# The gated group formed second in two mixer passes, and smaller portions of beside-work

## The chip, the cores and the metric

One core of a Trainium2 chip runs the whole program in one launch. The metric is the device time in microseconds (us) of that core; lower is better. A core has five engines with queues of their own: TensorE (PE in the profile, with its weight loads as PEld), VectorE (DVE), ScalarE (ACT), GpSimd (POOL) and SyncE (SP), which here only issues DMAs. Each engine takes its instructions strictly in the order of its queue.

## The reference

One layer of a hybrid encoder over 2048 prompt tokens and 32 tokens of a running stream. Cut to what matters here:

```python
h = rms_norm(x, g_mix); p = h @ w_in            # 1024 -> 2048 columns, eight groups of 256
ya = pool_mixer(seg[0], ...)                    # trailing windows 2/4/8/16, mean - self
z  = seg[1] * sigmoid(seg[2])                   # the gated group ("glu")
c  = causal_depthwise(z, w_dw, 31 taps) + b_dw
yb = silu(layer_norm(c))
yc = seg[4] * causal_depthwise(seg[5] * seg[3], w_sconv, 3 taps)
yd = seg[6] * chunk_mlp(seg[7])                 # v: mixed over positions in chunks of 128
x  = x + concat(ya, yb, yc, yd) @ w_out
x  = x + (silu(f @ w_gate) * (f @ w_up)) @ w_down     # f = rms_norm(x, g_ffn)
y  = rms_norm(x, g_final)
```

All numbers are fp32. A product of two fp32 numbers is formed from a high and a low part of each, with three matmuls.

## The kernel before, in words

**Tiles.** The 2080 tokens are five chunks (`c` = 0 to 4) of `C` = 416. The mixers run in three passes over them, `PASSES = ((0,), (1, 2), (3, 4))`; p is the pass. Then comes the feed-forward part, which the change does not touch. A *product* is one output tile of 128 columns by 416 tokens: 8 slices of the 1024 inputs, three matmuls each (L230 hi·whi, L231 hi·wlo, L232 lo·whi). The mixers have 120 products: 80 of the input projection, and 40 of `w_out`. I number them P0 to P119 in the order in which TensorE does them; pass 1 starts with P16, its products go chunk by chunk. A group of columns is two products per chunk (four in passes 1 and 2; `in_short`, `in_glu` have two pairs, so eight). Each weight of 128 columns is loaded by SP (L136), cut into `whi` by ACT (L137) and `wlo` by POOL (L138); three such pairs fit.

**Groups.** In passes 1 and 2 each group is a function: `in_v` (the last group, and the start of the generator `spatial`: transposes `tp` L620, ACT copies `vt` L624, matmuls `mx` L631, DVE sums L645), `in_short`, `in_pool` (starts `pooling`), `in_glu` (the gated group: sigmoid `g` L571 on ACT, product `z` L574 on DVE; then the generator `taps`), and `in_gates` (which takes up the results of the others). Before, pass 1 has the order v, short, pool, glu, gates, that is P16–19, P20–27, P28–31, P32–39, P40–47; then `w_out` of pass 0 is P48–55. Pass 2 has v P56–59, pool P60–63, glu P64–71, short P72–79, gates P80–87; then come `w_out` of pass 1 (P88–103) and of pass 2 (P104–119).

**Beside-work.** Generators hold the work that is not a matmul of a product: `taps(p, z)` (60 instructions of DVE at L726, 30 taps for each of two tiles, 128x416 in pass 0, 128x832 in pass 1 and 128x862 in pass 2), `normed_silu` (per chunk, after the taps: sum `sm` L738 on DVE, `total` L742 on PE, L746 on DVE, squares on ACT L755, `tok` L147 on PE, `ms` on DVE, a power `rt` L163 on POOL, then, in passes 0 and 1, a round trip through DRAM, `line` L185 and `rs` L187 on SP's queue, then L773 on DVE and the silu L776 on ACT), `pooling`, `short_conv`, `stats(c)` (loads of `xt`, L791, and their squares on ACT, L794: what the norm of chunk c needs), `normed(c)` (forms the chunk's `hi` and `lo`, loading `xk`, L436; DVE's are L211 and L207, ACT's L214), and for `w_out` `mixed_parts`. After every product `fill(budget)` runs steps of the first three started generators, and after them of `spare`, where the taps are; each step has a cost, and `fill` stops when the budget is spent. `need(...)` runs a generator to its end on the spot.

**Order.** DVE and PE do their instructions in the order in which the program writes them (`MANUAL`); those of ACT, POOL and SP are put in an order by the scheduler when the kernel is built. So `fill` and `need` set how much of the taps stands between which products in DVE's queue, and where PE's `total`, `tok` and `mx` stand between products.

**What ties glu to the taps.** The gated `z` has one buffer, so `in_glu(p)` begins with `need(("taps", p - 1))`: what is left of the taps of the pass before goes into DVE's queue in one piece. `w_out_pass` adds each product to `x2` on DVE (L376); `ps` has five buffers, so PE can be four products ahead of DVE. `ps_ax`, for the small matmuls, has three.

Of the kernel before, what the change touches and what calls it, by code (L numbers as in the profile page):

```python
# [79 lines left out]
def width(p, h):  # L80
    n0, n1 = tail(p)
    return h + n0 + (h + n1 if n1 else 0)
# [3 lines left out]
def trunk_kernel(ctx: ExitStack, tc: tile.TileContext, a):  # L86
# [40 lines left out]
    def weight(pool, src, lo_eng, cuts=1, between=None, raw=None):  # L127
        hi = pool.tile([P, KT, P], F32R, tag="whi", name="whi")
        lo = pool.tile([P, KT, P], F32R, tag="wlo", name="wlo")
        hf, lf = (t.rearrange("p k m -> p (k m)") for t in (hi, lo))  # L130
        if raw is None:
            raw = wts.tile([P, D], F32, tag="raw", name="raw", bufs=2)
        n = D // cuts
        for q in range(cuts):
            o = slice(q * n, (q + 1) * n)
            nc.sync.dma_start(out=raw[:, o], in_=src[:, o])  # L136
            nc.scalar.copy(out=hf[:, o], in_=raw[:, o])  # L137
            lo_eng.tensor_sub(out=lf[:, o], in0=raw[:, o], in1=hf[:, o].bitcast(F32))  # L138
            if between:
                between(q)  # L140
        return hi, lo
# [96 lines left out]
    def ktiles(pair):  # L238
        hi, lo = pair
        return [(hi[:, k], lo[:, k]) for k in range(KT)]  # L240
# [18 lines left out]
    def fill(budget):  # L259
        budget -= debt[0]  # L260
        late = []
        i = 0
        while budget > 0 and i < min(active[0], len(ahead)):
            step = next(ahead[i], DONE)
            if step is DONE:
                ahead.pop(i)
            elif step is WAIT or step is LATE:
                if step is LATE:
                    late.append(ahead[i])
                i += 1  # L270
            else:
                budget -= step
        while budget > 0 and spare:
            step = next(spare[0], DONE)
            if step is DONE:
                spare.pop(0)
            elif step is WAIT:
                break
            else:
                budget -= step  # L280
        for g in late:
            while (step := next(g, DONE)) is not WAIT:
                if step is DONE:
                    ahead.remove(g)
                    break
                budget -= step
        debt[0] = max(-budget, 0.0)
# [3 lines left out]
    def need(*names):  # L291

        for name in names:
            for _ in made[name]:
                pass

    def start(name, gen, spot=None):
        made[name] = gen
        ahead.insert(len(ahead) if spot is None else spot, gen)
# [63 lines left out]
    def w_out_pass(p, then=()):  # L363
        chunks = PASSES[p]
        order = (4, 5, 6, 7, 0, 1, 2, 3)
        for m0 in range(0, KT, 2):
            w = {m: ktiles(weight(wts, a["w_out"][m], nc.gpsimd)) for m in (m0, m0 + 1)}
            for c in chunks:
                need(("mixed", c))
                for m in w:  # L370
                    ps = ps_mm.tile([P, 512], F32, tag="mm", name="ps")
                    product(ps[:, :C], [w[m][k] for k in order], [mh[c][k] for k in order])
                    if (c, m) in then:
                        then[c, m]()
                    fill(3.7)
                    nc.vector.tensor_add(out=x2[c][:, m], in0=ps[:, :C], in1=x2[c][:, m])  # L376
            yield

    with ExitStack() as st:
# [99 lines left out]
        def project(p, h, *ms, w=None, pre=(), then=()):  # L479

            w = dict(w or {})
            for m in ms:
                if m not in w:
                    w[m] = ktiles(weight(wts, a["w_in"][m], nc.gpsimd))
            for c in PASSES[p]:
                if c:
                    need(("h", c))
                for m in ms:
                    if (c, m) in pre:
                        ps = pre[c, m]  # L490
                    else:
                        ps = ps_mm.tile([P, 512], F32, tag="mm", name="ps")
                        product(ps[:, :C], w[m], h[c])
                        if (c, m) in then:
                            then[c, m]()
                        fill(2.8 if p == 0 else 3.7)
                    yield c, m, ps[:, :C]

        def in_v(p, products):
            chunks = PASSES[p]  # L500
            n0, n1 = tail(p)
            v = segp.tile([P, 2, HV + width(p, 0)], F32, tag="seg", name="v", bufs=2)
            if chunks[0] * C % P:
                halo(v, "v", HV, p)
            for c, m, ps in products:
                o = HV + (c - chunks[0]) * C
                plain(v[:, m - 14, o : o + C], ps, c)
            keep(v, "v", HV, p)
            if n1:
                nc.scalar.dma_start(out=a["o_v"], in_=v[:, :, HV + n0 :])  # L510
            for c in chunks:
                mix[c] = bigp.tile([P, KT, C], F32, tag="big", name="mix")
            start(("spatial", p), spatial(p, v))
# [41 lines left out]
        def in_glu(p, h, **pre):  # L555
            if p > 1:
                need(*(("normed", c) for c in PASSES[p - 2]))
            if p:
                need(("taps", p - 1))
            z = segp.tile([P, 2, width(p, 30)], F32, tag="z", name="z")  # L560
            halo(z, "conv", 30, p)
            for t in range(2):
                for c, m, ps in project(p, h, 4 + t, 2 + t, **pre):
                    if m >= 4:
                        g = row("g")
                        if c == 0:
                            times_r(g, ps, c)
                            nc.scalar.activation(out=g, in_=g, func=AF.Sigmoid)
                            times_r(g, g, c)
                        else:  # L570
                            nc.scalar.activation(out=g, in_=ps, func=AF.Sigmoid)  # L571
                        continue
                    for s, d, n in conv_pieces(p, 30, c):
                        nc.vector.tensor_mul(  # L574
                            out=z[:, t, s : s + n], in0=ps[:, d : d + n], in1=g[:, d : d + n]
                        )
            states(z, "conv", 30, p)
            made["taps", p] = taps(p, z)
            spare.append(made["taps", p])

        def in_pool(p, h):
            need(("pooling", 1) if p == 2 else ("spatial", p))
            pz = segp.tile([P, 2, width(p, 15)], F32, tag="seg", name="pz", bufs=2)
            halo(pz, "pool", 15, p)
            for c, t, ps in project(p, h, 0, 1):
                for s, d, n in conv_pieces(p, 15, c):
                    if c == 0:
                        nc.vector.tensor_mul(
                            out=pz[:, t, s : s + n], in0=ps[:, d : d + n], in1=rfirst[:, d : d + n]
                        )  # L590
                    else:
                        nc.scalar.copy(out=pz[:, t, s : s + n], in_=ps[:, d : d + n])
            states(pz, "pool", 15, p)
            start(("pooling", p), pooling(p, pz))
# [187 lines left out]
        h = {}  # L782
        rt = {}

        def stats(c):

            rt[c] = rowp.tile([P, NTB], F32, tag="rt", name="rt", bufs=6)
            for js in ((0, 1, 2), (3,)):
                xt = bigp.tile([P, KT * C], F32, tag="big", name="xt")
                for i, j in enumerate(js):  # L790
                    nc.sync.dma_start(out=xt[:TB, i * D : (i + 1) * D], in_=a["xt"][c, j])  # L791
                for i, j in enumerate(js):
                    xj = xt[:TB, i * D : (i + 1) * D]
                    nc.scalar.activation(out=xj, in_=xj, func=AF.Square, accum_out=rt[c][:TB, j : j + 1])  # L794
                    yield WAIT
            rsqrt_of([rt[c][:TB]], 1.0 / D, rt=rt[c])
            yield WAIT
# [40 lines left out]


        in_v(1, project(1, h, 14, 15))  # L840
        start(("stats", 3), stats(3))
        in_short(1, h)
        start(("stats", 4), stats(4))
        in_pool(1, h)
        in_glu(1, h)
        need(("pooling", 0), ("normed", 0), ("stats", 3), ("stats", 4))
        in_gates(1, h, {
            (1, 13): lambda: (start(("mixed", 0), mixed_parts(0), 0), start(("h", 3), normed(3), 0)),
# [3 lines left out]


        in_v(2, project(2, h, 14, 15))
        in_pool(2, h)
        in_glu(2, h)
        in_short(2, h)
        whole.add(0)
        start(("fstats", 0), ffn_stats(0))
# [795 lines left out]
```

## Time and profile before

| | |
|---|---|
| time, median of 3 runs | 2127.08 us (2125.25 to 2128.69) |
| profiled execution | 2125.5 us; its span in the trace 2123.8 us |
| busy share of the span | PE 95%, PEld 93%, DVE 68%, POOL 54%, ACT 36% |
| mean granted TensorE clock | 0.982 |
| mixers, 0 to about 658 us | of 117 to 658 us PE is busy 519 us |
| feed-forward, 658 to 2124 us | PE busy 1415.5 of 1466 us |

The profile shows one execution. Its times count from the start of the span. The views used below are: the timeline (start, length, engine, line, operation, tiles, number of instructions; in square brackets how long the engine had been idle and what ended it), the list of waits, groups of instructions (busy time, mean of one, idle time before), the chain of work that ended last, and the table of stretches (for each: busy us of PE, PEld, DVE, ACT and POOL with the number of instructions, then the granted clock, the DMA share, GB/s).

### The profile page before, as it was taken

What the parts mean: (1) busy time and instruction counts of PE and PEld (TensorE: products, weight loads), DVE (VectorE), ACT (ScalarE), POOL (GpSimd) and SP (SyncE); (2) the same over time, 40 slices, a digit from 0 to 9 for tenths busy, and PEclk for the clock granted to TensorE, in tenths of its full rate; (3) what the DMA queues carried; (4) which work ended last, traced back from release to release, by engine and by line L of the source; (5) the groups of instructions that cost most, each with busy time, mean ns of one, the idle gap of its engine ahead of it and who ended that gap; (6) DMA issues with size and microseconds to landing.
All of it is one profiled execution on the core that took longest, in us unless ns stands there. A gap on an engine that the chain in (4) does not pass through costs nothing.

```text
span 2123.8 us, 31916 instructions
## 1 busy us (share of the span) xinstructions
PE 2027.5 (95%) x11902; PEld 1980.8 (93%) x11902; DVE 1444.6 (68%) x2207; ACT 767.5 (36%) x1472; POOL 1138.5 (54%) x891
## 2 busy tenths in 40 slices
PE   8699998999997999999999999999999999999997
PEld 7689997899897999999998999999998999999997
DVE  3896599499576677556557676787557577656555
ACT  5423232332334333333334343333334333333332
POOL 2523352243335655656668565666667556655664
PEclk9899998999998999999999999999999999999998
DMA  7634233113367445222224534543224534422221
GB/s 214 177 94 112 71 116 112 41 61 124 108 168 206 137 136 153 85 71 78 78 99 146 188 97 128 159 151 124 75 86 148 195 103 136 133 70 75 75 80 59
DMA packets 152011, 247.88 MB, mean 117 GB/s; under 512 B 23440, under 2 KB 101008, under 8 KB 151216
## 3 DMA queue, kind: packets, MB, share of 16 engines
q1 hardware_dynamic: 149136, 245.67, 37.4%
q8 instruction: 94, 1.54, 0.3%
q14 instruction: 61, 0.50, 0.1%
q10 hardware_dynamic: 2720, 0.18, 0.1%
HBM read 209.42 MB, written 36.36 MB: 116 GB/s over the span
## 4 chain that ended last, share of the span: by engine, by line
PE 51%; DVE 18%; issue 11%; POOL 10%; DMA 7%; ACT 2%; SPq 1%; POOLq 0%; DVEq 0%; ACTq 0%
PE pw L1136 8%; PE pw L1134 8%; PE pw L1135 8%; DVE cv L726 6%; POOL wlo L1020 6%; PE pd L1150 5%; PE pd L1149 5%; PE pd L1151 5%; PE ps L230 4%; PE ps L232 4%; PE ps L231 3%; POOL dlo L1277 2%; DMA line<-rt 2%; DMA xk<-in_x 1%; POOL f_p L963 1%
## 5 line engine op out<-in xcount | busy, mean ns | idle before, releaser
L1136 PE MATMUL pw<-f_p,whi 128*128 128x346 f32 (+1 forms) x1848 | 598.4, 324 | 10.6 <-POOL f_p L963 10.5
L1134 PE MATMUL pw<-f_p,whi 128*128 128x346 f32 (+1 forms) x1848 | 597.5, 323 | 9.0 <-DVE sg L1227 6.0
L1135 PE MATMUL pw<-f_p,wlo 128*128 128x346 f32 (+1 forms) x1848 | 596.3, 323 | 0.0
L1020 POOL TENSOR_TENSOR wlo<-sum,whi 128x512 fp32r<-128x512 f32 x264 | 354.6, 1348 | 288.7 <-ACT whi L1019 285.7
L1152 DVE TENSOR_TENSOR xs<-pd,xs 128x346 f32<-128x346 f32 (+1 forms) x528 | 262.7, 512 | 240.3 <-PE pd L1151 240.2
L1136 PEld LDWEIGHTS pw<-f_p,whi 128*128 128x128 f32 x1848 | 350.1, 189 | 13.6 <-POOL f_p L963 13.6
L1134 PEld LDWEIGHTS pw<-f_p,whi 128*128 128x128 f32 x1848 | 351.5, 190 | 11.7 <-issue 8.3
L1135 PEld LDWEIGHTS pw<-f_p,wlo 128*128 128x128 f32 x1848 | 350.3, 190 | 0.3 <-POOL wlo L1020 0.3
L1277 POOL TENSOR_TENSOR dlo<-raw,dhi 128x256 fp32r<-128x256 f32 x256 | 223.0, 891 | 227.3 <-ACT dhi L1276 224.6
L1149 PE MATMUL pd<-hhi,dhi 128*128 128x346 f32 (+1 forms) x1024 | 330.4, 323 | 15.0 <-DVE xs L1152 15.0
L1150 PE MATMUL pd<-hhi,dlo 128*128 128x346 f32 (+1 forms) x1024 | 329.7, 322 | 0.1
L138 POOL TENSOR_TENSOR wlo<-raw,whi 128x1024 fp32r<-128x1024 f32 x67 | 183.9, 2749 | 269.9 <-ACT whi L137 268.1
L1151 PE MATMUL pd<-hlo,dhi 128*128 128x346 f32 (+1 forms) x1024 | 328.5, 321 | 0.0
L1020 POOL TENSOR_TENSOR wlo<-raw,whi 128x512 fp32r<-128x512 f32 x199 | 275.4, 1392 | 36.6 <-ACT whi L1019 36.4
L1019 ACT CAST whi<-sum 128x512 fp32r<-128x512 f32 x264 | 163.8, 621 | 295.7 <-DVE sum L1054 106.4
L230 PE MATMUL ps<-hi,whi 128*128 128x416 f32 x640 | 236.0, 369 | 8.5 <-ACT hi L214 4.1
L231 PE MATMUL ps<-hi,wlo 128*128 128x416 f32 x640 | 229.5, 359 | 6.6 <-POOL wlo L138 6.0
L232 PE MATMUL ps<-lo,whi 128*128 128x416 f32 x640 | 230.9, 361 | 3.2 <-POOL lo L207 3.0
L726 DVE SCALAR_TENSOR_TENSOR cv<-z,par,cv 128x416 f32<-128x416 f32 (+2 forms) x180 | 216.4, 1263 | 1.0 <-ACT cv L720 0.9
L1149 PEld LDWEIGHTS pd<-hhi,dhi 128*128 128x128 f32 x1024 | 192.8, 188 | 19.8 <-DVE xs L1152 19.2
L1150 PEld LDWEIGHTS pd<-hhi,dlo 128*128 128x128 f32 x1024 | 192.5, 188 | 1.9 <-POOL dlo L1277 1.5
L1151 PEld LDWEIGHTS pd<-hlo,dhi 128*128 128x128 f32 x1024 | 193.0, 189 | 0.0
(185 smaller groups left out, 2863.0 us busy)
## 6 DMA issues: line engine op xcount, KB each, us to landing
raw<-in_w_up SPq DMA_DIRECT2D x132, 256.0 KB
raw<-in_w_gate SPq DMA_DIRECT2D x128, 256.0 KB
raw<-in_w_down SPq DMA_DIRECT2D x256, 128.0 KB
raw<-in_w_in SPq DMA_DIRECT2D x43, 512.0 KB
raw<-in_w_out SPq DMA_DIRECT2D x24, 512.0 KB
f_p<-td SPq DMA_DIRECT2D x14, 692.0 KB
xt<-in_xt SPq DMA_DIRECT2D x20, 416.0 KB
x<-in_x SPq DMA_DIRECT2D x5, 1664.0 KB
```

The costliest lines, as they stand in the source:

```text
L230: nc.tensor.matmul(out, whi, xhi, start=start and k == 0, stop=False)
L231: nc.tensor.matmul(out, wlo, xhi, start=False, stop=False)
L232: nc.tensor.matmul(out, whi, xlo, start=False, stop=stop and k == n - 1)
L726: nc.vector.scalar_tensor_tensor(out=cv[:, t, :n], in0=z[:, t, j : j + n], scalar=col("w_conf", 31 * t + j), in1=cv[:, t, :n], op0=ALU.mul ...
L1020: nc.gpsimd.tensor_sub(out=lf, in0=src, in1=hf.bitcast(F32))
L1134: nc.tensor.matmul(ps, whi[:, k], xhi[:, k, :n], start=start and k == 0, stop=False, **more)
L1135: nc.tensor.matmul(ps, wlo[:, k], xhi[:, k, :n], start=False, stop=False, **more)
L1136: nc.tensor.matmul(ps, whi[:, k], xlo[:, k, :n], start=False, stop=stop and k == H - 1, **more)
L1149: nc.tensor.matmul(ps, whi, hhi[:, :n], start=i == 0, stop=False)
L1150: nc.tensor.matmul(ps, wlo, hhi[:, :n], start=False, stop=False)
L1151: nc.tensor.matmul(ps, whi, hlo[:, :n], start=False, stop=i == 1)
L1277: nc.gpsimd.tensor_sub(out=lf, in0=raw, in1=hf.bitcast(F32))
```

## The change

`fill` in `w_out_pass` and in the projections of passes 1 and 2 gets 3.3 in place of 3.7. Pass 1 goes v, glu, short, pool, gates, and pass 2 goes v, glu, pool, short, gates. `stats(3)` and `stats(4)` keep their places beside `in_short`, so `stats(3)` now starts after `in_glu(1)`. The flush `need(("taps", 0))` thus stands after P19 in place of P31, and `need(("taps", 1))` after P59 in place of P63. The glu products are P20–27 and P60–67 after the change; short is P28–35 and P72–79, pool is P36–39 and P68–71.

```diff
@@ w_out_pass, L375
-                    fill(3.7)
+                    fill(3.3)
@@ project, L496
-                        fill(2.8 if p == 0 else 3.7)
+                        fill(2.8 if p == 0 else 3.3)
@@ the passes, L838 to L858
         in_v(1, project(1, h, 14, 15))
+        in_glu(1, h)
         start(("stats", 3), stats(3))
         in_short(1, h)
         start(("stats", 4), stats(4))
         in_pool(1, h)
-        in_glu(1, h)
...
         in_v(2, project(2, h, 14, 15))
+        in_glu(2, h)
         in_pool(2, h)
-        in_glu(2, h)
         in_short(2, h)
```

What moves is seen in the engines' queues. **First place: the start of pass 1.** On DVE, after the last low part of chunk 2 (`lo_962`), the 26 taps that stood before the first sums of `spatial` become 41, and `sm` follows at once (before):

```order
L207 TENSOR_TENSOR lo_962<-f_1030,hi_961 128x416
L726 SCALAR_TENSOR_TENSOR cv_641<-z_326,par_80,cv_641 128x416 x26
L645 TENSOR_TENSOR mix_1104<-mx_1190,bsb_112 64x2x96 x2
L528 TENSOR_TENSOR zs_1106<-ps_1165,xs_1163 128x416
L726 SCALAR_TENSOR_TENSOR cv_641<-z_326,par_80,cv_641 128x416 x5
```

The same place in the queue after:

```order
L207 TENSOR_TENSOR lo_962<-f_1031,hi_961 128x416
L726 SCALAR_TENSOR_TENSOR cv_641<-z_326,par_80,cv_641 128x416 x41
L738 TENSOR_TENSOR sm_1174<-cv_641 128x416
L746 SCALAR_TENSOR_TENSOR cv_641<-total_1208,cv_641 128x416 x2
L645 TENSOR_TENSOR mix_1103<-mx_1210,bsb_112 64x2x96 x2
L574 TENSOR_TENSOR z_1135<-ps_1183,g_1181 128x416
```

On PE the matmul `total`, which reads that `sm`, stood before between P26 and the `mx` that follows it:

```order
L232 MATMUL ps_1393<-lo_962,whi_1296 128x416
L742 MATMUL total_1418<-sm_1380,ones_87 128x416
L631 MATMUL mx_1420<-wst_111,vt_1388 128x256 x2
L620 MATMUL tp_1423<-ident_82,v_922 96x128 x2
L230 MATMUL ps_1439<-hi_961,whi_1302 128x416
```

After, it stands between P21 and P22, five products earlier:

```order
L232 MATMUL ps_1183<-lo_478,whi_1143 128x416
L742 MATMUL total_1208<-sm_1174,ones_87 128x416
L631 MATMUL mx_1210<-wst_111,vt_1179 128x2x96 x2
L620 MATMUL tp_1213<-ident_82,v_922 128x128 x2
L230 MATMUL ps_1228<-hi_961,whi_1137 128x416
```

**Second place: ACT between P22 and P28.** Before, the copies `vt` of `spatial` are in front of the squares L794 of `xt`, or behind three of them (`vt_1388`, which `mx` needs after P26):

```order
L448 COPY xs_1353<-ps_1308 128x416
L624 COPY vt_1339<-tp_1336 128x256
L794 ACTIVATE xt_1519,rt_1518<-xt_1519 104x1024 x3
L624 COPY vt_1388<-tp_1385 128x256
L794 ACTIVATE xt_1626,rt_1518<-xt_1626 104x1024
L539 ACTIVATE mix_1104<-zs_1106,par_80 128x416
L137 CAST whi_1480<-raw_1482 128x1024
L755 ACTIVATE q0_1430<-cv_641 128x416
L624 COPY vt_1426<-tp_1423 96x256
```

After, the three squares `xt_1515` of chunk 3 come right before `vt_1396`, which `mx` needs after P26; then come the fourth, three of chunk 4, the two silu of chunk 0 and two loads of a function table before `vt_1436`, which `mx` needs after P27:

```order
L794 ACTIVATE xt_1515,rt_1514<-xt_1515 104x1024 x3
L624 COPY vt_1396<-tp_1393 128x256
L794 ACTIVATE xt_1614,rt_1514<-xt_1614 104x1024
L776 ACT_TABLE_LOAD
L776 ACTIVATE mix_325<-cv_641,par_80 128x416 x2
L794 ACTIVATE xt_1798,rt_1797<-xt_1798 104x1024
L720 ACTIVATE cv_1520<-z_1135,par_80 128x832
L794 ACTIVATE xt_1798,rt_1797<-xt_1798 104x1024
L571 ACT_TABLE_LOAD
L571 ACTIVATE g_1440<-ps_1401 128x416
L137 CAST whi_1483<-raw_1485 128x1024
L794 ACTIVATE xt_1798,rt_1797<-xt_1798 104x1024
```

The row behind the last of these is `vt_1436`, the copy L624 of 96x256.

On SP, in whose order the transfers start, the `xt` loads after the change stand behind the round trip of chunk 0 (`line_1347` waits for POOL's `rt`):

```order
L136 DMA raw_1485<-in_w_in 128x1024
L185 DMA line_1347<-rt_1305 104x4x1
L187 DMA rs_1349<-line_1347 128x416
L136 DMA raw_1623<-in_w_in 128x1024
L791 DMA xt_1515<-in_xt 104x1024 x3
```

And in pass 0 SP had the first three `xt` of chunk 3 (`xt_1151`) among the `xk` loads of chunk 1; they are no longer there. Before:

```order
L791 DMA xt_820<-in_xt 104x1024
L791 DMA xt_1151<-in_xt 104x1024
L436 DMA xk_536<-in_x 128x416
L136 DMA raw_559<-in_w_in 128x1024
L436 DMA xk_542<-in_x 128x416
L791 DMA xt_1151<-in_xt 104x1024 x2
L436 DMA xk_592<-in_x 128x416
```

**Third place: DVE in `w_out` of pass 0.** Before, each sum into `x2` has three or four taps of 128x832 behind it:

```order
L726 SCALAR_TENSOR_TENSOR cv_1952<-z_1632,par_80,cv_1952 128x832 x3
L376 TENSOR_TENSOR x2_2154<-ps_2273,x2_2154 128x416
L726 SCALAR_TENSOR_TENSOR cv_1952<-z_1632,par_80,cv_1952 128x832 x3
L376 TENSOR_TENSOR x2_2154<-ps_2315,x2_2154 128x416
L726 SCALAR_TENSOR_TENSOR cv_1952<-z_1632,par_80,cv_1952 128x832 x4
L376 TENSOR_TENSOR x2_2154<-ps_2344,x2_2154 128x416
L726 SCALAR_TENSOR_TENSOR cv_1952<-z_1632,par_80,cv_1952 128x832 x3
```

After there are two or three, and 16 in place of 20 in front of the first `f` of chunk 4; four are left for later, where there were 20:

```order
L726 SCALAR_TENSOR_TENSOR cv_1520<-z_1135,par_80,cv_1520 128x832 x2
L376 TENSOR_TENSOR x2_2174<-ps_2287,x2_2174 128x416
L726 SCALAR_TENSOR_TENSOR cv_1520<-z_1135,par_80,cv_1520 128x832 x3
L376 TENSOR_TENSOR x2_2174<-ps_2334,x2_2174 128x416
L726 SCALAR_TENSOR_TENSOR cv_1520<-z_1135,par_80,cv_1520 128x832 x3
L376 TENSOR_TENSOR x2_2174<-ps_2363,x2_2174 128x416
L726 SCALAR_TENSOR_TENSOR cv_1520<-z_1135,par_80,cv_1520 128x832 x3
```

## The prediction

> **What bounds the kernel now.** I read the page first, then the table of stretches, then PE's waits and the timeline of the engines that PE waits for. PE is busy 95% of the span, so time is won or lost only where PE stands still or runs at a lower clock. The feed-forward part is not touched; the mixers end at about 658 us. PE's waits from 117 us on:
>
> ```profile
> PE pp L672 <- DVE sa L700: 4.8, 2, 4.2
> PE ps L230 <- ACT hi L214: 4.1, 4, 1.8
> PE ps L232 <- POOL lo L207: 3.0, 3, 2.3
> PE ps L230 <- DVE x L376: 2.9, 1, 2.9
> PE total L742 <- DVE sm L738: 2.9, 1, 2.9
> PE ps L232 <- DVE mlo L314: 2.1, 2, 1.5
> ```
>
> They are few and nearly all are DVE behind with the taps, or what follows from DVE (`hi`, `lo` of a chunk). A product without waits and the worst stretch of the mixers, in the table of stretches:
>
> ```profile
> 243.66:279.92 36.26, 36.26 (x193) 35.93 (x192) 34.31 (x30) 8.45 (x9) 11.42 (x5) 1.00 0.20 59
> 313.34:345.36 32.02, 24.32 (x98) 20.68 (x98) 30.17 (x33) 7.09 (x12) 10.04 (x5) 0.79 0.41 140
> ```
>
> Eight products take 36.26 us, 4.53 each, at a granted clock of 1.00. The second row holds four (P55 to P58), which should take 18.1 and take 32.0: 13.9 are lost, part as waiting, part as the clock of 0.79 after the waits. I price every wait of several us with 1.5 us for that slower stretch behind it.
>
> DVE in pass 1, from the end of chunk 2's `lo`:
>
> ```profile
> 134.86 0.59 DVE L207 TENSOR_TENSOR lo<-f,hi 128x416 fp32r<-128x416 f32 x1
> 135.36 19.12 DVE L726 SCALAR_TENSOR_TENSOR cv<-z,par,cv 128x416 f32<-128x416 f32 x26
> 155.66 2.90 DVE L726 SCALAR_TENSOR_TENSOR cv<-z,par,cv 128x416 f32<-128x416 f32 x5
> 137.53 2.42 POOL L138 TENSOR_TENSOR wlo<-raw,whi 128x1024 fp32r<-128x1024 f32 x1 [4.86 <-ACT whi L137]
> 142.07 2.40 POOL L138 TENSOR_TENSOR wlo<-raw,whi 128x1024 fp32r<-128x1024 f32 x1 [0.34 <-ACT whi L137]
> ```
>
> Five taps take 2.90, 0.565 each with the overlap of neighbours. 26 of them would be 14.7, but took 19.12: two weight subtractions of POOL lie in them, and each costs DVE about 2.2.
>
> **The change, part by part.** Minus is time saved.
>
> *A, the flush before glu(1): +15.5.* At 135.36 there are now 41 taps in one piece, then `sm`. With the same two subtractions: 19.12 + 15 x 0.565 = 27.6, so to 163.0, and `sm` to 163.5. `total` stands on PE right behind P21. PE at that place before:
>
> ```profile
> 149.64 0.81 PE L631 MATMUL mx<-wst,vt 128*128 128x192 f32 x4
> 177.59 0.86 PE L742 MATMUL total<-sm,ones 128*128 128x416 f32 x2
> 178.29 1.03 PE L631 MATMUL mx<-wst,vt 128*128 128x256 f32 x4
> 189.12 0.81 PE L147 MATMUL tok<-ones,q 128*104 128x1 f32 x8
> ```
>
> P21 ended at 149.6, so PE stands still for 13.9, and 1.5 to 1.6 follow at the lower clock. Before, the same taps were hidden by P20 to P26, and `total` at 177.59 waited for nothing. Bounds: without the two subtractions in it 12; with two more 19. I take the middle, as POOL's two subtractions serve the weight buffers that P18 and P19 free, in both kernels.
>
> *B, `vt` behind the squares of `xt`: +11.* ACT takes its queue in order, and the squares wait for loads:
>
> ```profile
> 164.96 1.66 SPq L791 DMA_DIRECT2D xt<-in_xt  x4
> 170.58 1.06 ACT L794 ACTIVATE xt<-xt 104x1024 f32<-104x1024 f32 x1 [1.59 <-DMA xt<-in_xt]
> 172.69 1.06 ACT L794 ACTIVATE xt<-xt 104x1024 f32<-104x1024 f32 x1 [0.96 <-DMA xt<-in_xt]
> 174.81 1.06 ACT L794 ACTIVATE xt<-xt 104x1024 f32<-104x1024 f32 x1 [0.96 <-DMA xt<-in_xt]
> 175.87 0.35 ACT L624 COPY vt<-tp 128x256 f32<-128x256 f32 x1
> 191.58 6.70 DMA line<-rt
> ```
>
> The first load lands 5.6 after its issue, the next ones 2.1 apart; `vt` was there at 176.2, 1.3 before `mx` wanted it behind `total`. After the change SP has the `xt` behind `line` and `rs` of chunk 0. From `tok` (189.12) to the issue of `line` (191.58) are 2.5, the line takes 6.7, `rs` and one weight load go out in 0.8: `xt` is issued 10 after `tok` and lands 15.6, 17.7 and 19.8 after it. `tok` now follows P23; P24, P25 and P26 with their `mx` and `tp` end 17.5 after it (3 x 5.63, the pitch of such products from 149.64 to 155.2, and 0.7). The third square and `vt_1396` are done 21.4 after `tok`: PE waits 3.9, and loses 1.5 at the lower clock. `vt_1436`, wanted one product later (28.5 after `tok`), is behind four more squares, a cast, a sigmoid and two table loads:
>
> ```profile
> 207.12 1.28 ACT L571 ACT_TABLE_LOAD   x1
> 208.42 0.52 ACT L571 ACTIVATE g<-ps 128x416 f32<-128x416 f32 x1
> ```
>
> With loads 2.1 apart the third `xt` of chunk 4 lands 28.2 after `tok`, and with the casts in between `vt_1436` is done at 31.8, a wait of 3.3; if that load has to wait until chunk 3's squares free the buffer, at 34.4, a wait of 5.9. I take 4.6, with 1.5 behind it. Sum 11.5, taken as 11; bounds 5 (the loads land 3 earlier, and only one wait of 3.5 is left) and 15 (buffer wait, and 2 more on the first load).
>
> By the Trainium skill ("ScalarE: Activation LUTs", section "What ACT_TABLE_LOAD costs") a switch is 1283 ns of load and 1380 ns of drain. The trace agrees with the load (1.28) and shows no drain behind it: the next activation starts 0.02 later. By the page B would be 2 x 1.4 = 2.8 more.
>
> *C, DVE's lag in `w_out` of pass 0 and chunk 4's `h`: -8.5.* Before:
>
> ```profile
> 303.70 0.58 DVE L376 TENSOR_TENSOR x<-ps,x 128x416 f32<-128x416 f32 x1
> 311.98 8.34 DVE L726 SCALAR_TENSOR_TENSOR cv<-z,par,cv 128x832 f32<-128x832 f32 x4
> 320.25 0.58 DVE L376 TENSOR_TENSOR x<-ps,x 128x416 f32<-128x416 f32 x1
> 320.75 3.06 DVE L726 SCALAR_TENSOR_TENSOR cv<-z,par,cv 128x832 f32<-128x832 f32 x3
> 331.70 0.58 DVE L376 TENSOR_TENSOR x<-ps,x 128x416 f32<-128x416 f32 x1
> 332.20 1.20 DVE L211 SCALAR_TENSOR_TENSOR f<-xk,par,rs 128x416 f32<-128x416 f32 x2
> 343.74 1.27 DVE L207 TENSOR_TENSOR lo<-f,hi 128x416 fp32r<-128x416 f32 x2
> ```
>
> The sum at 331.70 is that of P54, which PE had finished at 313.34: DVE is 18.4 behind. So P56 waits for a free `ps` (the sum at 320.25), and chunk 4's `lo`, done at 345.0, holds up P58. A tap of 832 is 1.0 (3 in 3.06), and 2.1 more with a subtraction in it (four in 8.34). In the queue after the change 16 taps stand in this pass in place of 20, and in gates(1) some taps give way to the pooling of pass 1; my sum of DVE's rows from P41 to P55 is 55.4 against 59.0. Counting on from P29, where the second run of taps starts, DVE has 94.7 of its own, and 40 of some 18 subtractions, against some 125 on PE: it is 10 behind at P54, 8.4 less than before. `lo` is then done 8.5 earlier against PE, and P56's wait is inside that. Bounds: the 3.6 from the rows alone, and 11 when two subtractions fewer fall into the taps.
>
> *D, pass 2 with glu before pool: 0.* 32 of the 60 taps of pass 1 are done beside short(1), and only four are left when glu(2) comes, so this flush costs nothing. The wait of `pp` for `sa` (4.2, and 2.6 at the lower clock) goes, since pooling has more room. In its place `mx` after P66 depends on a `vt` behind four silu, which need the `rs` of two chunks:
>
> ```profile
> 395.32 0.16 DVE L157 TENSOR_SCALAR ms<-tok 104x4 f32<-104x4 f32 x1 [4.55 <-PE tok L147]
> 203.05 1.36 ACT L776 ACTIVATE mix<-cv,par 128x416 f32<-128x416 f32 x2 [6.64 <-DVE cv L773]
> 418.80 1.09 DVE L773 TENSOR_TENSOR cv<-rs,cv 128x416 f32<-128x416 f32 x2 [9.34 <-DMA rs<-line]
> ```
>
> The second chunk's L773 thus came 23.5 after the first `ms`. After the change `tok` stands behind P62, and `mx` wants its `vt` four products with their `mx` and `tp` later, 0.8 + 4 x 5.63 = 23.3. The `vt` is there 0.3 + 23.5 + 1.1 (L773) + 1.4 (two silu) + 1.1 to 2.5 (the first step of the taps and, by ACT's queue, a table) + 0.4 = 27.8 to 29.2 after `tok`: PE waits about 5.2 and loses 1.5, against 6.8 saved. Bounds -3 and +3.
>
> *F, `w_out` of pass 1: 0.* The waits for `mlo` (2.1) and for `sm` (2.9, and 1.5 behind it) go, since DVE is less late and `total` stands one product later. But `tok` now stands right in front of `rb`, where one product (P99) was between: the way `tok`, `ms`, `rt` (1.4), a weight subtraction on POOL (2.4), the second `rt`, `dg`, `rb` takes some 6.4, open to PE, with 1.5 behind it. Bounds -3 and +3. The start of the feed-forward part I leave at +0.5: its taps and sums end before P117 as before.
>
> *E, pass 0 without the loads of chunk 3: -3.* The chain of work runs early on through a load of chunk 1:
>
> ```profile
> 47.05 7.36 DMA xt<-in_xt
> 54.48 14.07 DMA xk<-in_x
> 68.57 0.65 DVE f L211
> ```
>
> Behind it DVE is the chain up to 113 us. Three `xt` of 0.43 MB leave the transfers there, 1.28 MB, which at the 216 to 250 GB/s of that stretch is 5.5 at most. One of the three stands before that `xk`, two start beside it. I take 3, between 0 and 5.5.
>
> Smaller portions as such cost nothing on PE: what is taken from `fill` stands later, beside products that wait for nothing (first row of the stretches); where that cover is gone the taps meet a `need`, which is D's flush of four taps, 4 us if PE had no lead.
>
> **Sum.** 15.5 + 11 - 8.5 + 0 + 0 + 0.5 - 3 = +15.5. Against the profiled execution's 2125.5 that is 2141; the median of the three runs lies 1.6 above it, so 2142 for a median.
>
> **The rivals.**
>
> 1. *The loads come in time (B is absent).* ACT's order puts three loads before `vt_1396`; if the transfers land 6 earlier than reckoned, no `mx` waits. Against it: before, `vt` made it by 1.3 only, with the loads issued without a round trip ahead of them. 2142 - 11 = 2131.
> 2. *The lag of DVE is worth more (the other side).* If all that PE loses to late taps goes, it is 13.9 (the second row of the stretches) + 6.8 (`pp`) + 2.1 + 4.4 (`mlo`, `sm`) = 27.2, where I count 8.5 with D and F at 0. Then A and B are outweighed: 15.5 + 11 - 27.2 - 3 = -3.7, and with B's lower bound -9.7: 2117 to 2123. It decides from 23 us of removed lag on. Against it: chunk 4's `xk` and the f's themselves hold P58 for part of the 13.9 however early DVE is.
> 3. *The new waits grow in pass 2.* L773 for two chunks blocks DVE's queue, with `z` and the sums of `spatial` behind it; at one more line round trip (6.7) D is +7: 2149.
> 4. *A table switch drains.* B is 2.8 more: 2145. The row at 208.42 speaks against it.
> 5. *The portions alone count, and the flush is hidden.* Needs 41 taps in 14.2 us (from 135.36 to 149.6), 0.35 each, where no row is under 0.56: 2127.
>
> **How the numbers follow.** A change of under 0.2%, 4.3 us, can't be told from none. Chances: my forecast (A and B, 2135 to 2146) 0.55; rival 1 0.15, half of it inside 0.2%; rival 2 0.07; rival 3 0.15; rival 4 0.03; rival 5 0.05. So faster 0.07, same 0.13, slower 0.80. The single bounds added in squares (A 3.5, B 5, C 4, D, F and E 3 each) give 9; the range reaches from 2126, below rival 1, to 2153, above rival 3.
>
> **What would show it.** A: 41 taps in one row on DVE and PE idle 12 to 16 us before `total`, released by `sm`. B: `mx` waiting twice for `vt` after P26 and P27, ACT idle for `xt` in front of it. C: P56 not waiting for L376, P58 ending some 23 us after P54 in place of 32. D: no wait of `pp` for `sa`, one of `mx` in glu(2). F: no wait for `mlo`, one of `rb` for `dg`. E: everything before P16 some 3 us earlier. I am wrong if `total` waits less than 8 us, or if pass 1 up to P40 is not at least 15 us longer.

## The result, and the profile after

The changed kernel takes 2152.86 us (median of 4 runs, 2151.69 to 2157.84), the kernel before 2127.48 beside it: a ratio of 1.0132, 95% interval 1.0117 to 1.0146. On the chip on which most of the experiments ran, it was 2151.76 against 2122.59, 1.0141 (1.0122 to 1.0161). The change makes the kernel slower by some 25 to 30 us; the prediction had 15, and its range ended at 2153, a ratio of 1.012.

PE's waits of the changed kernel from 117 us on (total, number, longest):

```profile
PE mx L631 <- ACT vt L624: 14.6, 3, 6.2
PE total L742 <- DVE sm L738: 13.8, 1, 13.8
PE rb L179 <- DVE dg L168: 6.4, 2, 4.5
PE ps L230 <- ACT hi L214: 6.0, 5, 2.7
PE ps L232 <- POOL lo L207: 3.1, 3, 2.3
PE ps L230 <- DVE x L376: 2.4, 1, 2.4
```

`pp` for `sa`, `mlo` and P56's wait for `x` are gone from the list; `vt`, `total` and `rb` have come in. The start of each product can be read from its first matmul of L230, and set against the product of the same number in the profile before (the groups differ, the length of a product does not). The steps of that difference, in us, for the profiled executions:

| products | after, minus before | after on the second chip | the kernel before on the second chip |
|---|---|---|---|
| to P20 (E) | -5.3 | -3.7 | +3.9 |
| P20 to P22 (A) | +16.3 | +16.3 | 0.0 |
| P22 to P29 (B) | +14.8 | +13.0 | 0.0 |
| P29 to P52 | -1.5 | -1.1 | -0.5 |
| P52 to P59 (C) | -4.5 | -4.3 | +0.1 |
| P59 to P78 (D) | -1.0 | -2.5 | -2.0 |
| P78 to P88 | 0.0 | 0.0 | +0.7 |
| P88 to P101 (F) | +2.0 | +1.8 | -1.5 |
| P101 to P119 | +2.5 | +2.4 | -0.2 |
| behind P119 | +2.7 | +2.0 | -0.4 |
| span | +26.0 | +23.9 | 0.0 |

The last column shows how far one kernel differs from itself: nearly 4 us in the first stretch, whose chain of work runs through loads, at most 2 in the others. So effects are read from the steps, and a difference of up to 4 us between two profiled spans is not read as an effect.

A, on DVE and PE of the changed kernel:

```profile
130.03 27.56 DVE L726 SCALAR_TENSOR_TENSOR cv<-z,par,cv 128x416 f32<-128x416 f32 x41
157.63 0.59 DVE L738 TENSOR_TENSOR sm<-cv 128x416 f32<-128x416 f32 x1
158.28 1.75 PE L742 MATMUL total<-sm,ones 128*128 128x416 f32 x2 [13.81 <-DVE sm L738]
```

41 taps in one row, 27.56 long, then `sm`, and PE idle for 13.81 in front of `total`. The prediction had 27.6 and 13.9. The row of the stretch shows what follows: a granted clock of 0.71.

```profile
139.68:161.38 21.70, 7.89 (x35) 6.69 (x34) 19.63 (x36) 1.42 (x4) 0.65 (x1) 0.71 0.09 25
185.07:215.50 30.43, 20.50 (x85) 18.89 (x84) 9.60 (x14) 17.71 (x27) 5.91 (x4) 0.78 0.72 214
```

The second row is B, P26 to P29 (start of the one to start of the other): three products in 30.43 us, at 0.78 of the clock, with transfers at 214 GB/s. ACT and SP there:

```profile
181.45 0.33 SPq L187 DMA_DIRECT2D rs<-line  x1
181.88 0.37 SPq L136 DMA_DIRECT2D raw<-in_w_in  x1
182.31 2.15 SPq L791 DMA_DIRECT2D xt<-in_xt  x4
195.80 1.61 SPq L791 DMA_DIRECT2D xt<-in_xt  x4
189.89 1.06 ACT L794 ACTIVATE xt<-xt 104x1024 f32<-104x1024 f32 x1 [9.74 <-DMA xt<-in_xt]
194.63 1.06 ACT L794 ACTIVATE xt<-xt 104x1024 f32<-104x1024 f32 x1 [0.43 <-DMA xt<-in_xt]
195.68 0.35 ACT L624 COPY vt<-tp 128x256 f32<-128x256 f32 x1
196.09 2.07 PE L631 MATMUL mx<-wst,vt 128*128 128x256 f32 x4 [6.22 <-ACT vt L624]
197.10 1.28 ACT L776 ACT_TABLE_LOAD   x1
198.40 1.36 ACT L776 ACTIVATE mix<-cv,par 128x416 f32<-128x416 f32 x2
200.12 1.06 ACT L794 ACTIVATE xt<-xt 104x1024 f32<-104x1024 f32 x1 [0.36 <-DMA xt<-in_xt]
207.45 1.65 PE L631 MATMUL mx<-wst,vt 96*128 96x192 f32 x4 [3.71 <-ACT vt L624]
SPq L791 <- ACT vt L624: 11.5, 1, 11.5
```

ACT stands for 9.74 us at the first square, with `vt` behind the third. The first load lands 7.6 after its issue, where the prediction took 5.6. Four loads are under way at that time, as in the kernel before. Chunk 4's four go out only at 195.80, when ACT has done the third square (SP waits 11.5 for it), and the first of them lands 4.2 after its issue. What differs is what SP issued just ahead: one weight load (L136) in the kernel before, `rs` and a weight load here, nothing in the 12 us ahead of chunk 4's. The weight load here landed 2.0 us later after its issue than the one before the change (6.0 against 3.9, by the landing marks in the traces), and the first `xt` 2.0 behind it in both.

The activation after the table load starts 0.02 us behind it, as before the change. The Trainium skill ("ScalarE: Activation LUTs", section "What ACT_TABLE_LOAD costs") has 1.38 us of drain with each switch; the row shows none here.

F, the last two chunks in front of P100:

```profile
574.04 1.54 PE L147 MATMUL tok<-ones,q 128*104 128x1 f32 x16
576.12 2.35 POOL L138 TENSOR_TENSOR wlo<-raw,whi 128x1024 fp32r<-128x1024 f32 x1
579.47 0.59 DVE L168 TENSOR_TENSOR dg<-ident,rt 104x416 f32<-104x416 f32 x1 [2.79 <-POOL rt L163]
580.12 1.76 PE L179 MATMUL rb<-dg,ones 104*128 104x416 f32 x2 [4.53 <-DVE dg L168]
581.98 1.09 DVE L773 TENSOR_TENSOR cv<-rb,cv 128x416 f32<-128x416 f32 x2 [1.92 <-PE rb L179]
583.71 1.73 PE L179 MATMUL rb<-dg,ones 104*128 104x416 f32 x2 [1.84 <-DVE dg L168]
```

The way is `tok`, `ms`, a weight subtraction on POOL between the two `rt`, `dg`, `rb`, as predicted; but it is gone over twice in part. In DVE's queue chunk 3's L773, which waits for the first `rb`, stands in front of chunk 4's `dg`, so the second `rb` waits for the first.

### The profile page after: what moved, and what is told of

Same layout as the page of the kernel before. It is cut to its first block, busy times and chain, and to the rows that moved or that the text cites. A ratio compares the mean times of both kernels' runs of the same rounds, so it can differ in the third digit from the quotient of the medians.

```text
span 2149.8 us, 31927 instructions
## 1 busy us (share of the span) xinstructions
PE 2033.8 (95%) x11902; PEld 1989.3 (93%) x11902; DVE 1441.3 (67%) x2207; ACT 768.6 (36%) x1472; POOL 1133.4 (53%) x891
## 4 chain that ended last, share of the span: by engine, by line
PE 42%; issue 10%; POOL 9%; DVE 8%; DMA 2%; ACT 2%; SPq 0%; POOLq 0%; DVEq 0%; ACTq 0%
PE pw L1136 8%; PE pw L1134 8%; PE pw L1135 8%; POOL wlo L1020 6%; PE pd L1150 5%; PE pd L1149 5%; PE pd L1151 5%; POOL dlo L1277 2%; POOL f_p L963 1%; DVE xs L1152 1%; DVE ssum L1349 1%; DMA xf<-away 1%; PE ps L230 1%; PE ps L232 1%; PE ps L231 1%
## 5 line engine op out<-in xcount | busy, mean ns | idle before, releaser
L138 POOL TENSOR_TENSOR wlo<-raw,whi 128x1024 fp32r<-128x1024 f32 x67 | 176.3, 2634 | 267.2 <-ACT whi L137 237.4
L230 PE MATMUL ps<-hi,whi 128*128 128x416 f32 x640 | 236.3, 369 | 7.2 <-ACT hi L214 6.0
L1149 PEld LDWEIGHTS pd<-hhi,dhi 128*128 128x128 f32 x1024 | 193.1, 189 | 19.8 <-DVE xs L1152 19.2
L726 DVE SCALAR_TENSOR_TENSOR cv<-z,par,cv 128x416 f32<-128x416 f32 (+2 forms) x180 | 208.3, 1218 | 0.1
```

The lines of the kernel that those rows point to most:

```text
L230: nc.tensor.matmul(out, whi, xhi, start=start and k == 0, stop=False)
L1149: nc.tensor.matmul(ps, whi, hhi[:, :n], start=i == 0, stop=False)
```

## The experiments

Each ran beside the kernel before on its own chip; times are set against that. The first four expectations in absolute times (B, A, the order, the portions) were written with 2127.5 for the kernel before, where it took 2121.9 to 2122.6 on those chips; they are read here as distances from the kernel before. The changed kernel is 29.2 above it on the second chip.

**The two kernels again.**

> The kernel before, unchanged, profiled once more on the chip of the experiments, as a scale for the stages. If the stages behave alike in every run, its products from P20 on lie where those of the first profile lie, but for a constant shift from the first 60 us, where the loads set the pace; I expect a shift of -2 to -5 us at P20, since this kernel's median here is 2121.9 us against 2127.5 us on the first chip. Rival: the difference between the chips is spread over the feed-forward part (clock), and P20 lies within 1 us.

> The changed kernel, unchanged, timed and profiled on the chip of the experiments, so that all single steps are measured against the same kernels. As on the first chip the ratio to the kernel before should be 1.012 to 1.014 (25 to 30 us).

The profiled execution of the kernel before took 2125.5 us, 0.8 above the slowest of its 18 other runs there (2116.1 to 2124.7); P20 came 3.9 later than in the first profile, not earlier, and all but 0.6 of that was made up by P101. So the expectation of an earlier P20 was wrong, and the way to P20 varies by as much as E is worth. E shows in one place of it: P9 to P11 takes 4.1 to 4.3 less than in the first profile in all nine profiled executions in which chunk 3's loads start later, and in the other four 0.1 to 2.0 more. The changed kernel behaved as on the first chip.

**B alone taken away.** The squares of chunks 3 and 4 are held behind the last `vt`:

```diff
             rt[c] = rowp.tile([P, NTB], F32, tag="rt", name="rt", bufs=6)
+            while c > 2 and made["spatial", 1].gi_frame:
+                yield WAIT
+            if c > 2:
+                nc.scalar.copy(out=rt[c][:1], in_=last_vt[0][:1, :NTB])
```

> The changed kernel with the squares of xt of chunks 3 and 4 put behind the last vt of spatial(1) on ACT, by a copy of four numbers from that vt into rt; the order of the loads on SP stays. If the squares in front of vt are what PE waits for after P26 and P27, both waits (6.2 and 3.7 us) and the slow clock behind them go, 13 to 14 us in all: 2138 to 2141 us. Rival: the waits come from the two table loads, the silu and the first step of the taps that stay in front of the last vt, so that only the first wait goes: 2143 to 2148 us.

Measured: 2141.61 us, 1.0092 (1.0068 to 1.0115), 10 us faster than the changed kernel on the same chip. That is 19.8 above the kernel before, where the expectation meant 10.5 to 13.5 and the rival 15.5 to 20.5; by the time alone the rival would stand. The steps and the waits decide against it (the added lines shift the line numbers):

```profile
PE total L744 <- DVE sm L740: 12.4, 1, 12.4
PE mx L633 <- ACT vt L625: 4.7, 1, 4.7
```

The one wait for `vt` that is left is in pass 2 (P66). P22 to P29 takes +0.3 in place of +14.8: both waits went, although the two table loads, the silu and the first step of the taps still stood in front of the last `vt`. The expected cause is shown, and the rival's is not what PE waited for. Not all of it reached the time, since this execution was 2.3 later than the changed kernel at P20 by the second column of the table, and lost 3 more behind P101.

**A taken away.** `total` of chunk 0 waits three products longer:

```diff
             yield WAIT
+            for _ in range(3 if p == 0 else 0):
+                yield WAIT
             total = ps_ax.tile([P, 512], F32, tag="ax", name="total")
```

> The changed kernel with three more waiting steps before total of chunk 0, so that total stands behind P24 and not behind P21; the flush of 41 taps stays on DVE. If A is PE waiting at total alone, PE goes on with P22 to P24 while DVE works off the taps; three buffers for the small matmuls then hold it before the fourth transpose for 2 to 5 us, so 10 to 13 us of the 13.8 and the 1.6 behind it go. In this build four squares of xt stand before the last vt and their loads go out ahead of line, so B goes too: 2125 to 2132 us. Rival: the flush holds PE in any case, through ps or ps_ax: 2137 us or more.

Measured: 2140.92 us, 1.0087 (1.0071 to 1.0103). Three of its waits on PE:

```profile
PE mx L631 <- ACT vt L624: 6.2, 1, 6.2
PE tp L620 <- DVE mix L645: 4.6, 1, 4.6
PE ps L231 <- POOL wlo L138: 4.3, 2, 2.7
```

No wait for `total`, and none for `vt` in pass 1: the 6.2 is that of pass 2. P20 to P29 costs +6.4 in place of +31.0; B goes with A here, as expected, since the first `xt` loads go out ahead of `line`. What is left of A is the transpose that waits for a buffer of `ps_ax`, as expected (4.6, and the clock behind it). But the time came out at the rival's side: 19.1 above the kernel before, where -2.5 to 4.5 were expected and 9.5 or more by the rival. New waits for weights came in (4.3, at P33 and P41; P29 to P52 +5.8 against -1.5), and P20 was 5.4 later against the kernel before than in the changed kernel's first profile, though P9 to P11 has E's gain. So A is PE waiting at `total`, and taking it away frees more than half of it (7.0 of 16.3 are left, P22 to P26); the expectation of the time was too low because I let nothing come after it.

**The order alone, and the portions alone.**

```diff
-                    fill(3.3)
+                    fill(3.7)
-                        fill(2.8 if p == 0 else 3.3)
+                        fill(2.8 if p == 0 else 3.7)
```

> The new order of the groups with the old portions (3.7 in both places). In this build total, tok and rb of the last two chunks stand one product apart again in w_out of pass 1, as before the change, so if the small portions are what sets them right behind each other, the wait for dg before P100 (8.9 and 2.0 us in the changed kernel) and the wait of P117 for x2 with the slow start of the feed-forward part (2.6 and 2.7) go, while DVE's lag in w_out of pass 0 grows again (by 1 to 3 us, four taps more): 2141 to 2145 us. Rival: the order alone makes the time and the portions cost nothing, as the prediction had it: 2151 to 2155 us.

Measured: 2140.91 us, 1.0089 (1.0074 to 1.0104). A and B are as in the changed kernel (+16.3, +15.0); from P88 to the end of the mixers it has -0.5 in place of +4.5, and behind P119 -1.3 in place of +2.7. No `rb` waits for `dg` and P117 does not wait, as expected. The time is 19.1 above the kernel before, nearer to the expected 13.5 to 17.5 than to the rival's 23.5 to 27.5, but outside both. `total` waits more often here:

```profile
PE total L742 <- DVE sm L738: 24.7, 4, 13.8
```

Three of the four were not forecast: two behind P55 (5.3 and 0.9) and one behind P94 (4.7).

The portions alone are the reverse: `fill(3.3)` in both places, the old order of groups.

> The old order of the groups with the small portions (3.3 in both places). In this build the sums of the last two chunks are not reached by the portions, and total, tok, dg and rb of both stand in one piece before P100. If small portions cost there, PE stands still for the whole way sm, total, L746, squares, tok, ms, rt, dg, rb, some 15 to 22 us, against 5 to 8 us of waits that go (P56, P88, P96): 2136 to 2144 us, slower than before. Rival: what is taken from the portions stands later beside products that wait for nothing: 2125 to 2129 us.

Measured: 2135.34 us, 1.0068 (1.0050 to 1.0085), 13.5 above the kernel before, as expected (8.5 to 16.5): the small portions alone make the kernel slower, and the rival, which was the prediction's own view, falls. The order alone costs 19.1, the portions alone 13.5, both together 29.2, a little less than their sum. Around P99:

```profile
553.72 1.56 PE L742 MATMUL total<-sm,ones 128*128 128x416 f32 x4
559.54 1.55 PE L147 MATMUL tok<-ones,q 128*104 128x1 f32 x8 [4.26 <-POOL q L756]
563.16 1.73 PE L179 MATMUL rb<-dg,ones 104*128 104x416 f32 x2 [2.07 <-DVE dg L168]
564.67 1.43 PE L147 MATMUL tok<-ones,q 128*104 128x1 f32 x8
568.16 1.73 PE L179 MATMUL rb<-dg,ones 104*128 104x416 f32 x2 [2.06 <-DVE dg L168]
```

`total`, `tok` and `rb` of both chunks stand in one piece, and between 553.7 and 569 PE does no product. P88 to P101 costs +5.0 although P88 to P99 takes 10.2 less, and the next stretch +2.4 as in the changed kernel. P52 to P59 gains 5.1.

**Only the portions of `w_out` of passes 1 and 2 undone.**

```diff
-                    fill(3.3)
+                    fill(3.3 if p == 0 else 3.7)
```

> The changed kernel with the portions of w_out of passes 1 and 2 back at 3.7; the projections and w_out of pass 0 keep 3.3. total stands one product earlier and tok and rb of the last two chunks are one product apart. If the small portions in these two passes are the cause of the wait for dg at P100 (8.9 and 2.0 us of product time) and of P117's wait for x2 (2.6), both go, against some 4 to 6 us that come back before P97 (total waits for sm again): 17 to 21 us above the kernel before, where the changed kernel is 25 to 28 above it. Rival: the waits come from DVE being late by the new order, and stay: 25 us or more above.

Measured: 2142.93 us, 1.0095 (1.0079 to 1.0110), 21 above the kernel before; expected 17 to 21. P88 to P101 is -4.3 in place of +2.0 and P101 to P119 -0.2 in place of +2.5: F and the wait of P117 come from the portions there, and the rival falls.

```profile
559.19 1.66 PE L742 MATMUL total<-sm,ones 128*128 128x416 f32 x4 [2.82 <-DVE sm L738]
576.25 1.67 PE L179 MATMUL rb<-dg,ones 104*128 104x416 f32 x4 [0.28 <-DVE dg L168]
```

Here `total` waits as before the change (2.82), and `rb` 0.28. Behind P119 this execution was 7.3 longer than the first profile; why is open.

**Chunk 4's `h` started two products earlier.**

```diff
-            for _ in w_out_pass(0, {(0, 5): lambda: start(("h", 4), normed(4), 0)}):
+            for _ in w_out_pass(0, {(0, 3): lambda: start(("h", 4), normed(4), 0)}):
```

> The changed kernel with chunk 4's normed started two products earlier in w_out of pass 0 (behind P51 in place of P53), so that six taps move behind its f's. P58 and P59 stand 8.9 us apart from where they should. If that wait is the lag of DVE when the f's start and the loads of xk behind the first three f's (14.4 us from the first f to the last lo), starting two products earlier takes 6 to 8 us of it: 18 to 22 us above the kernel before. Rival: the f's then wait for rs or xk, or hold up the sums into x2, and P55 or P56 waits instead: less than 3 us won, 23 to 27 above.

Measured: 2157.94 us, 1.0169 (1.0154 to 1.0184), slower than the changed kernel. P58 took 4.0 less than in the kernel before, but P56 and P57 4.6 more, so that P52 to P59 came out at -4.2, as in the changed kernel (-4.5); and P60 took 8.2 more. PE's waits there:

```profile
PE total L742 <- DVE sm L738: 18.8, 2, 13.8
PE ps L230 <- ACT whi L137: 3.6, 1, 3.6
```

The taps that the f's passed came back as a second wait for `sm`, behind P60 (18.8 less the 13.8 of A). P57 waited for a weight (3.6 for `whi`, 1.7 more for `wlo`), not for `rs`, `xk` or `x`. So moving the f's in the queue moved the loss: that fits a DVE with too much to do in this stretch, but no run shows it by itself. The rival was right that less than 3 us would be won; its mechanism was not seen, and the time, 36 above the kernel before, is outside its 23 to 27.

**Three parts in the old order.** The portion of `w_out` of pass 0 alone:

```diff
-                    fill(3.7)
+                    fill(3.3 if p == 0 else 3.7)
```

> The kernel before with one part of the change alone: portions of 3.3 in w_out of pass 0, 3.7 elsewhere, old order. If C is this portion, P56's wait for x2 (3.1 and 1.5) goes and P58's wait stays as it is, 3 to 5 us faster than the kernel before. Rival: the two taps that move behind chunk 4's f's come back as a longer wait in pass 2 (total or pp): no difference beyond 2 us.

Measured: 2120.30 us against 2122.59, 0.9997 (0.9983 to 1.0011): no difference. P52 to P59 gains 2.2, of which 1.4 lie at P52, where a wait for weights went; P56 still waits 2.5 for `x`. So this portion alone is not C. The rival has the time right, but its longer wait in pass 2 did not come (P59 to P78 -1.8).

`stats(3)` alone behind `in_short(1)`:

> The kernel before with stats(3) alone started behind in_short(1), so that the three loads of xt of chunk 3 leave the early stretch, and nothing else moves. If E is these loads, P10 to P20 come 4 to 5 us earlier than before and stay so: 3 to 5 us faster than the kernel before. Rival: the loads come back as a wait for vt in pass 1 (the squares of chunk 3 stand in front of a vt there), or the early stretch differs between runs by as much: no difference beyond 1.5 us.

Measured: 2123.00 us against 2121.86, 1.0009 (1.0000 to 1.0019): nothing won. P9 to P11 takes 4.3 less, as in the changed kernel; P27 to P29 gives 3.7 back, where the squares of chunk 3 now stand in front of a `vt` (`mx` waits 1.9 for it). The rival was right: E is real, and here it is paid for by a piece of B.

Both of these with 3.3 in pass 1 as well, and chunk 4's `normed` two products earlier:

> The old order of the groups, with three parts that the runs point to: stats(3) behind in_short(1), portions of 3.3 in pass 1 and w_out of pass 0 and 3.7 behind, chunk 4's normed two products earlier. By the sum of the steps seen so far: -4 (E), -5 (P55 to P59 in the run of the small portions alone), -5 to -7 (P58): 12 to 16 us faster than the kernel before. Rival: the gains overlap, since all three come out of the same wait at P56 to P58: 6 to 9 us faster.

Measured: 2135.56 us, 1.0063 (1.0046 to 1.0080), slower. The gains did not add: P59 to P78 took 5.2 more and P57 waited 6.7 for weights, much as in the run with `normed` earlier alone, and P29 to P52 took 6.3 more, with a wait of 3.7 for a weight at P33.

The last one grades the portions:

```diff
-                    fill(3.7)
+                    fill(3.3 if p == 0 else 3.9)
-                        fill(2.8 if p == 0 else 3.7)
+                        fill((2.8, 3.7, 3.5)[p])
```

> The old order with portions graded by stage: 3.7 in pass 1, 3.3 in w_out of pass 0, 3.5 in pass 2, 3.9 in w_out of passes 1 and 2, so that DVE carries fewer taps where it is late and the last two chunks' total, tok and rb stay one product apart. The waits of P56 (4.6) and part of those of P88 to P96 (8) go: 4 to 8 us faster than the kernel before. Rival: fewer taps in pass 2 only move the wait for sm to P97: 2 to 4 us faster, as the portion in w_out of pass 0 alone.

Measured: 2131.97 us, 1.0057 (1.0033 to 1.0081), slower. Up to P101 it was 6.6 us ahead of the first profile, of which 2.0 came by P20; then it lost 11.7 at P113 to P118, where weights came late; why they did is open:

```profile
PE ps L230 <- ACT whi L137: 4.8, 1, 4.8
PE ps L231 <- POOL wlo L138: 4.7, 2, 2.4
```

No version here beats the kernel before by more than the measurement can tell.

## Why the prediction was right or wrong

The direction and the two waits that make it were right; the size was 10.5 us short (15.5 against 26.0 in the trace). The step that failed above all is the sentence that smaller portions cost nothing on PE: with the new order kept and the old portions put back, 19.1 us above the kernel before are left of 29.2, and the portions alone cost 13.5. By terms, the end is 4.7 over the forecast, C 4.0, B 3.8, F 2.0 and A 0.8; D, P29 to P52 and E give 4.8 of this back, so part of the miss is hidden.

- **A, 15.5:** 16.3 measured. The bounds of 12 and 19 were not needed: the two subtractions fell into the taps as before, and each holds up one tap (2.79 and 2.82 long, where the other 39 take 0.64 to 0.73).
- **B, 11:** 14.8. The mechanism is shown by its removal (+0.3). The step that failed is the landing of the first load, taken as 5.6 from a row behind one weight load. I counted `rs` and the weight load ahead of it as 0.8, the time of their issue; with both ahead the first `xt` took 7.6, and the first wait was 6.2 in place of 3.9. The second was 3.7, near the lower of the two values I had (3.3 and 5.9), but by luck: chunk 4's loads did wait for chunk 3's squares, which was the case of the higher value, and then landed 4.2 after their issue, with nothing ahead of them. The pitch of 5.63 is that of P22 to P26; the rows named for it give 5.56.
- **C, -8.5:** -4.5, and of that 1.7 is a wait for weights at P52 that I had not counted. The sum of DVE's rows gave a lag of 10 at P54. It was 14.0:

```profile
349.89 0.58 DVE L376 TENSOR_TENSOR x<-ps,x 128x416 f32<-128x416 f32 x1
355.75 0.65 DVE L211 SCALAR_TENSOR_TENSOR f<-xk,par,rs 128x416 f32<-128x416 f32 x1 [2.40 <-DMA xk<-in_x]
```

P54 ended at 335.9, and its sum was made at 349.9; then chunk 4's fourth f waited 2.4 for its load. So P56's wait went, and P58's stayed (13.4 where it was 11.8). The lower bound of 3.6, from the rows alone, was nearer than the value I took, and without P52 the gain of 2.8 is below it. The lag at P54, 18.4 before, is 12.5 with the order alone, 14.4 with the portions alone and 16.9 with the portion of `w_out` of pass 0 alone: the parts do not add.
- **D, 0:** -1.0. `mx` waited 4.7 for `vt` (5.2 forecast), `pp` no longer for `sa`.
- **F, 0:** +2.0. The waits that go gave 8.8, where the forecast's terms make 6.5 (2.1 + 2.9 + 1.5). The new way cost 10.8 and not 7.9 (6.4 + 1.5), because the flush goes chunk by chunk and the second `rb` stands behind the first one's L773; an order that I had before me in DVE's rows and did not follow.
- **The end, +0.5:** 5.2, namely P117's wait for `x` (2.4) and 2.7 behind P119. P117's wait comes with the portions: it is there with the portions alone (+2.4) and gone when they are undone in `w_out` of passes 1 and 2 (-0.2). In front of P117 DVE works in one piece on the input of the feed-forward part up to 667.5, and only then makes four sums in a row (667.41, 2.07 long); with these portions undone that piece ends 3.8 before P117 starts. That the 2.7 behind P119 come from them too is not shown: the run with these portions undone had 7.3 there.
- **E, -3:** -5.3 by P20, but the kernel before differs from itself by 3.9 there; from P9 to P11 alone -4.3, and at least -4.1 in every execution with the later loads. The bound of 5.5 for these loads should be 5.9: 1.28 MB at 216 GB/s.

Rival 1 and rival 2 (27 us of lag removed) did not happen; the run with chunk 4's `h` started earlier suggests why rival 2 could not, since the taps moved there came back as other waits. Rival 3's time of 2149 is nearer to the result than the forecast, but its mechanism did not come: D is -1.0 and not +7. Neither of the two signs of being wrong that the prediction ends with came: `total` waited 13.8, and P40 starts 21.4 later than before (27.5 later counted from P16).

What stays open: the time on the second chip grew by 29 us and the span of the profiled execution by 24. The profiled execution lies above the other runs of the kernel before there, and at the lower end for the changed one, and the early stretch differs by 4 us, but that this is all of it was not shown. Open too is what sets the time behind P119, where the changed kernel and its variants differ from the first profile by -1.3 to +7.3.

## What to carry to other kernels

When a step that begins by flushing unfinished side work is moved earlier, count what is still unfinished there, at its measured pace, against the work that stands in front of the next instruction that needs it; that gave A's wait to 0.1 us (13.9 against 13.81). A smaller share of side work beside each product is not free: find the next point at which the rest is forced, and look at what waits there. On a queue in order, look for an instruction that waits for a late load in front of one that is wanted soon; holding the squares behind the last `vt` took away 14.5 of B's 14.8 us. And price a load by what was issued just ahead of it, not only by its own size.

## What was not expected of the hardware

In four more executions of kernels whose pass 0 is written as in the kernel before, P20 came between 2.0 earlier and 3.9 later than in the first profile. From P20 to P119 the two profiles of the kernel before agree within 0.3 us in 91 of 99 steps from product to product; the other eight differ by 0.5 to 2.3, and no cause is known for these.

In pass 1 the first of a row of four or six `xt` loads landed the later the more had been issued just ahead of it. By the landing marks in the profiled executions it took 3.8 to 4.2 us with nothing ahead (five cases), 5.5 to 6.1 behind a weight load alone (nine), and 7.3 to 9.7 behind `rs` and a weight load (seven). The length of the row did not show: two of the nine have six loads; this is `stats(3)` alone behind `in_short(1)`, where the first `xt` was there 5.5 after its issue:

```profile
161.14 0.33 SPq L136 DMA_DIRECT2D raw<-in_w_in  x1
161.52 2.68 SPq L791 DMA_DIRECT2D xt<-in_xt  x6
167.06 1.06 ACT L794 ACTIVATE xt<-xt 104x1024 f32<-104x1024 f32 x1 [0.95 <-DMA xt<-in_xt]
```

No run tested this by itself.
